# Weights of the second layer split into parts in the first, and attention scores with the other sign

## The chip, the cores and the metric

The kernel runs on one core of one Trainium2 chip. The metric is the device time of one execution in microseconds; before the change it is 2969.87 us, the median of 3 runs (2965.07 to 2971.68).

## The reference, cut to what matters

One inference step of a hybrid decoder: a layer with a Mamba-2 mixer and an MLP, then a shared projection to keys and values, then a layer with attention and an MLP. There are 1104 tokens in one pass: 1024 of a prompt, 64 of samples (8 sequences of 8) and 16 meta tokens; the second layer has 1088, without the meta tokens. All inputs are fp32.

```python
D_MODEL = 1024; D_FF = 4096; WINDOW = 128        # 16 query heads of 64, 4 key/value heads

def sq_relu_mlp(h, norm_w, w_up, w_down):
    return h + jnp.square(jax.nn.relu(rmsnorm(h, norm_w) @ w_up)) @ w_down

def shared_kv(h, kv_norm_w, w_kv):
    return (rmsnorm(h, kv_norm_w) @ w_kv)         # split into keys and values

def queries(h, norm_w, w_q):
    return (rmsnorm(h, norm_w) @ w_q)

def sink_softmax(scores, mask, sinks):            # one learned score per head beside the keys
    s = jnp.where(mask, scores, -jnp.inf)
    return jax.nn.softmax(jnp.concatenate([s, sink], axis=-1), axis=-1)[..., :-1]

# layer 0: h = h + mamba_mixer(h); h = sq_relu_mlp(h, ...)
# layer 1: hp = hp + swa_prompt(q_p, k_p, v_p, ...) @ w_o   (scores = q k * 64 ** -0.5, window of 128)
#          hs = hs + swa_sample(...) @ w_o ; h = sq_relu_mlp(h, ...) ; final rmsnorm
```

## The kernel before

**Products of fp32.** TensorE (PE) multiplies a rounded form of fp32 (fp32r). For full precision each operand is held as two such parts, high and low, and `mm3` (L174) issues three matmuls for each slice of 128: high by high, high by low, low by high (L179, L180, L181). The activations stay in SBUF as parts. The weights come from DRAM as units of 128x1024 numbers (512 KB), and each use of a unit makes its parts anew. `wunit` (L156) does this: a raw tile is loaded by a DMA of the SP queue (L160), GpSimd (POOL) multiplies it with the weights of the norm where the unit has them (L162), ScalarE (ACT) casts it to the high part (L164), and POOL subtracts that from the raw tile, which gives the low part (L165). Raw tiles come from a ring of 2 (L168), part tiles from a ring of 6 (L172), which the whole kernel shares.

**First layer, MLP.** After the mixer and two pairs of columns of the plain kind (`plain_up`, L858), `up` (L972) runs over 14 pairs `f` of column blocks of w_up. Each pair goes through Strassen's scheme, 7 products instead of 8 (`up_pair`, L913): `up_weights` (L894) loads two raw units, forms sums and differences on VectorE (DVE, L900, L906) and splits each of the seven into parts with `wparts` (L887: ACT L890, POOL L891), one slot of the ring of 6 for each. One raw tile in three comes from a slot of its own (`raw2`, L880). Then come one plain `down_block` and `down_blocks` (L1034): four blocks `b` of rows of w_down, each with four column blocks `p` of seven products `i`; between the products `step` loads and splits what the next block needs.

**Second layer, attention.** Keys and values are made from 4 units of w_kv (`keys`, L1186, `values`, L1220), with a raw load, a multiplication, a cast and a subtraction each. `attention` (L1414) then goes over three chunks of tokens, two pairs of heads `pr` and four `r`: `queries` (L1269) multiplies one unit of w_q, so that each of the 8 units is loaded and split three times, once a chunk; `attn_block` (L1313) handles 128 queries of two heads. In it PE makes the scores of each head in `sc`, DVE scales them by `rsq`, adds the mask and takes the maximum with the sink in one instruction (L1328, which writes `es` and, as an accumulator, the maximum into `few`). `soft` (L1295) changes the sign of the maxima (L1300, DVE, 128x2), ACT takes the exponentials with the negative maximum as bias and sums them (L1302), DVE takes the reciprocal (L1303) and multiplies (L1306); PE transposes the result, DVE and ACT copy it out of PSUM (`mb` L1343, `pb` L1345), PE multiplies with the values (`yb`), and ACT and DVE split the result into parts `ah` and `al` (L1356, L1357). `out_unit` (L1478) multiplies the attention output with units of w_o, 8 units three times each; DVE adds the product to the stream (L1490 from PSUM, L1491 from SBUF). At the end come the second layer's first two pairs of w_up, again by `plain_up` with `wunit`, then `up` and `down_blocks` as before.

**What sets the order.** The program is written as loops, and the framework's scheduler orders the instructions of all engines by its own estimate of their times. Each engine then takes its instructions in that order, and so does the SP queue that issues all the DMAs: an instruction that waits for a slot or a result holds all behind it on its engine.

## Time and profile before

| | |
|---|---|
| median of 3 runs | 2969.87 us (2965.07 to 2971.68) |
| profiled execution | 2972.13 us |
| its span, first to last instruction | 2970.4 us |
| mean granted clock of TensorE | 0.982 |
| busy: PE, DVE, ACT, POOL | 2848.8, 1945.4, 1452.5, 1419.9 us |

The stages in the profiled execution, in us from the start of the span: mixer and the first plain columns up to 1107, `up` of the first layer to 1407, its plain `down_block` to 1455 and `down_blocks` to 1722; keys and values 1725 to 1830, attention to 2211, the last output units and the start of the second MLP to 2300, and the rest of that MLP to the end.

The clock given for a stretch is the mean of what PE was granted in it, 1.00 being 2.4 GHz. "Busy" of PE counts overlapping matmuls once. Behind a group of instructions stands the idle time of its engine just before them, with the instruction that ended most of it.

### The profile page before, as it was taken

The numbers are of one execution on the slowest core, as the hardware profiler recorded it, in microseconds if no ns is written. First come the engines' busy times: TensorE is split into PE (matmuls) and PEld (weight loads), VectorE is DVE, ScalarE is ACT, GpSimd is POOL, SyncE is SP. The second block draws the span as 40 slices with busy tenths as digits, with TensorE's granted clock in tenths as the row PEclk, the third lists the DMA queues.
The fourth block names the chain that finished last, engine by engine and source line by source line (L and its number), as shares of the span: only waits on it lengthen the run. The fifth ranks groups of instructions, "written<-read, shape, count | busy, mean of one in ns | idle before, by whom it ended". The sixth has DMA issues, their size and how long they took to land.

```text
span 2970.4 us, 50898 instructions
## 1 busy us (share of the span) xinstructions
PE 2848.8 (96%) x19751; PEld 2733.9 (92%) x19751; DVE 1945.4 (65%) x3150; ACT 1452.5 (49%) x2771; POOL 1419.9 (48%) x1251
## 2 busy tenths in 40 slices
PE   8999999989999989999999999998988999999998
PEld 6999999979999989999999998887878999999998
DVE  6788777775646665453666766776788545366675
ACT  6555555555544554545333336555655444433333
POOL 5566666663223134444355555464543444435562
PEclk9999999999999999999999999998998999999999
DMA  4344444443212224445433312132233344543332
GB/s 134 97 127 125 123 123 124 132 128 117 65 58 88 82 81 158 136 151 181 189 129 129 119 43 65 59 93 89 88 108 103 133 140 145 192 167 127 132 108 75
DMA packets 195609, 346.38 MB, mean 117 GB/s; under 512 B 26712, under 2 KB 128984, under 8 KB 192792
## 3 DMA queue, kind: packets, MB, share of 16 engines
q1 hardware_dynamic: 195368, 343.14, 36.0%
q8 instruction: 155, 2.54, 0.4%
q14 instruction: 86, 0.70, 0.1%
HBM read 252.93 MB, written 91.12 MB: 116 GB/s over the span
## 4 chain that ended last, share of the span: by engine, by line
PE 37%; DVE 12%; DMA 5%; ACT 4%; issue 4%; POOL 3%; DVEq 0%; ACTq 0%; POOLq 0%; SPq 0%
PE g L179 4%; PE g L180 4%; PE g L181 4%; PE mc L179 2%; PE mc L181 2%; PE mc L180 2%; PE ma L179 2%; PE ma L180 2%; PE ma L181 2%; DMA t_e<-rx 2%; POOL w L891 2%; PE md L181 2%; PE md L180 2%; PE md L179 2%; PE mb L180 2%
## 5 line engine op out<-in xcount | busy, mean ns | idle before, releaser
L165 POOL TENSOR_TENSOR w<-raw,w 128x1024 fp32r<-128x1024 f32 x140 | 352.9, 2523 | 437.5 <-ACT w L164 355.3
L179 PE MATMUL g<-S,w 128*128 128x384 f32 (+2 forms) x1584 | 535.3, 338 | 14.1 <-DVE hh L761 4.8
L180 PE MATMUL g<-S,w 128*128 128x384 f32 (+2 forms) x1584 | 534.5, 337 | 0.1
L181 PE MATMUL g<-S,w 128*128 128x384 f32 (+2 forms) x1584 | 531.1, 336 | 2.0 <-POOL w L165 2.0
L891 POOL TENSOR_TENSOR w<-s,w 128x384 fp32r<-128x384 f32 (+1 forms) x240 | 321.7, 1343 | 396.7 <-ACT w L890 394.7
L891 POOL TENSOR_TENSOR w<-raw,w 128x384 fp32r<-128x384 f32 (+1 forms) x180 | 227.6, 1267 | 228.0 <-ACT w L890 205.0
L179 PEld LDWEIGHTS g<-S,w 128*128 128x128 f32 x1584 | 302.1, 191 | 18.9 <-DVE hh L761 5.1
L181 PEld LDWEIGHTS g<-S,w 128*128 128x128 f32 x1584 | 302.2, 191 | 3.5 <-POOL w L165 2.3
L180 PEld LDWEIGHTS g<-S,w 128*128 128x128 f32 x1584 | 302.3, 191 | 1.8 <-issue 0.7
L890 ACT CAST w<-s 128x384 fp32r<-128x384 f32 (+1 forms) x240 | 134.4, 562 | 233.4 <-PE ma L181 82.0
L179 PE MATMUL ma<-S,w 128*128 128x276 f32 (+1 forms) x736 | 214.6, 292 | 9.8 <-DVE us L1091 6.6
L180 PE MATMUL ma<-S,w 128*128 128x276 f32 (+1 forms) x736 | 213.7, 290 | 0.9 <-DVE S L855 0.9
L181 PE MATMUL ma<-S,w 128*128 128x276 f32 (+1 forms) x736 | 213.7, 290 | 0.0
L164 ACT CAST w<-raw 128x1024 fp32r<-128x1024 f32 x140 | 146.4, 1046 | 106.1 <-PE g L180 40.6
L568 DVE SCALAR_TENSOR_TENSOR fm<-xp,cv,fm 128x1024 f32<-128x1024 f32 x96 | 161.1, 1680 | 33.1 <-ACT fm L549 32.5
L761 DVE TENSOR_TENSOR hh<-hh,g 128x384 f32<-128x384 f32 (+2 forms) x264 | 134.4, 531 | 68.6 <-PE g L181 68.1
L890 ACT CAST w<-raw 128x384 fp32r<-128x384 f32 (+1 forms) x180 | 100.3, 561 | 148.7 <-PE mc L181 49.1
L179 PEld LDWEIGHTS ma<-S,w 128*128 128x128 f32 x736 | 139.9, 190 | 11.3 <-issue 5.2
L180 PEld LDWEIGHTS ma<-S,w 128*128 128x128 f32 x736 | 140.0, 190 | 1.1 <-DVE S L855 1.1
L181 PEld LDWEIGHTS ma<-S,w 128*128 128x128 f32 x736 | 139.8, 190 | 0.0
L179 PE MATMUL mc<-S,w 128*128 128x276 f32 (+1 forms) x464 | 134.6, 290 | 2.1 <-DVE hh L1091 1.3
L181 PE MATMUL mc<-S,w 128*128 128x276 f32 (+1 forms) x464 | 134.0, 289 | 0.0
(483 smaller groups left out, 8944.6 us busy)
## 6 DMA issues: line engine op xcount, KB each, us to landing
raw<-in_w_up_dram SPq DMA_DIRECT2D x64, 512.0 KB
raw<-in_w_in_dram SPq DMA_DIRECT2D x48, 512.0 KB
raw<-in_w_downs_dram SPq DMA_DIRECT2D x64, 384.0 KB
ab<-acs_d SPq DMA_DIRECT2D x64, 256.0 KB
S<-t_d SPq DMA_DIRECT2D x18, 828.0 KB
S<-t_e SPq DMA_DIRECT2D x18, 816.0 KB
t_d<-rx SPq DMA_DIRECT2D x12, 1104.0 KB
t_e<-rx SPq DMA_DIRECT2D x12, 1088.0 KB
```

The lines of the kernel that those rows point to most:

```text
L164: nc.scalar.copy(out=wh, in_=raw)
L165: nc.gpsimd.tensor_tensor(out=wl, in0=raw, in1=wh.bitcast(F32), op=ALU.subtract)
L179: mm(out=out, lhsT=wh, rhs=xh, start=(first and k == 0), stop=False)
L180: mm(out=out, lhsT=wh, rhs=xl, start=False, stop=False)
L181: mm(out=out, lhsT=wl, rhs=xh, start=False, stop=(k == n - 1))
L568: nc.vector.scalar_tensor_tensor(out=acc[:, :SEQ], in0=xp[:, k:k + SEQ], scalar=cv[:, j, k:k + 1], in1=acc[:, :SEQ], op0=ALU.mult, op1=ALU ...
L761: nc.vector.tensor_tensor(out=hv, in0=hv, in1=pt[:, :n], op=ALU.add)
L890: nc.scalar.copy(out=t[:, 0], in_=src)
L891: nc.gpsimd.tensor_tensor(out=t[:, 1], in0=src, in1=t[:, 0].bitcast(F32), op=ALU.subtract)
```

## The change

Two things are changed. First, 24 units of the second layer (8 of w_q, 4 of w_kv, the first 4 of w_up, 8 of w_o) are made into parts once, in the first layer's MLP: `split_ahead` calls `wunit` for the next unit of a list, and writes both parts to DRAM. It is called 14 times in `up`, after each pair, and 10 times in `down_blocks`, after the last product of the first three column blocks of a block, as long as the list lasts. In the second layer `wunit` loads both parts into slots of the ring of 6, in two DMAs of 512 KB, and does nothing else; there are 56 such uses. Second, the scores are computed with the other sign: `rsq`, the scale of the sample's scores and the sink are negative, the mask sum takes the minimum, and the exponential has a scale of -1, so that the minimum is already the bias. The instruction of L1300 is gone (68 times).

```diff
-    def wunit(self, view, a, b, pre=None, to=None):
-        nc = self.nc
+    def wunit(self, view, a, b, pre=None, to=None, key=None):
+        nc = self.nc
+        if key in self.split:
+            ws = [self.wtile([P, a, b]) for _ in range(2)]
+            for e, w in enumerate(ws):
+                nc.sync.dma_start(out=w.bitcast(F32), in_=self.split[key][:, e].rearrange("p (a b) -> p a b", b=b))
+            return ws
         raw = self.raw([P, a, b])
...
         return wh, wl
+    def split_ahead(self, n=1):
+        nc = self.nc
+        for key, view, pre in self.ahead[:n]:
+            a = view.shape[1]
+            b = 1024 // a
+            if pre is not None:
+                pre = self.ncol(pre).rearrange("p (k o) -> p k o", o=1).broadcast_to([P, a, b])
+            ws = self.wunit(view, a, b, pre)
+            d = self.dram.tile([P, 2, 1024], F32, name="ws_%s" % "_".join(map(str, key)))
+            for e, w in enumerate(ws):
+                nc.sync.dma_start(out=d[:, e].rearrange("p (a b) -> p a b", b=b), in_=w.bitcast(F32))
+            self.split[key] = d
+        self.ahead = self.ahead[n:]
...
-    def plain_up(self, layer, fp, chs, rd, rs=None, pre=None):
-        nc = self.nc
-        ws = [self.wunit(self.i["w_up"][layer, 2 * fp + e], KT, P, pre) for e in range(2)]
+    def plain_up(self, layer, fp, chs, rd, rs=None):
+        nc = self.nc
+        ws = [self.wunit(self.i["w_up"][layer, 2 * fp + e], KT, P, key=("up", 2 * fp + e) if layer else None)
+              for e in range(2)]
         for c in chs:
...
                 self.up_pair(layer, f, rd, rt)
+                self.split_ahead()
                 if f == 8:
...
                     step(b, p, i)
+                    if i == 6 and p < 3:
+                        self.split_ahead()
...
         nc.sync.dma_start(out=sraw, in_=i["attn_sinks"].broadcast_to([P, 16]))
-        nc.vector.tensor_copy(out=self.sink, in_=sraw.rearrange("p (c h r) -> p c r h", c=2, h=2))
+        nc.vector.tensor_scalar(out=self.sink, in0=sraw.rearrange("p (c h r) -> p c r h", c=2, h=2), scalar1=-1.0,
+                                scalar2=None, op0=ALU.mult)
...
         ks = self.ks[pr] = ap.tile([P, 80], F32, name="ks%d" % pr)
-        wh, wl = self.wunit(i["w_kv"][pr], KT, P, pre=self.kvn)
+        wh, wl = self.wunit(i["w_kv"][pr], KT, P, key=("kv", pr))
         for c, (o, n) in enumerate(CH):
...
         ds = slice(pr * P, pr * P + P)
-        wh, wl = self.wunit(i["w_kv"][2 + pr], KT, P, pre=self.kvn)
+        wh, wl = self.wunit(i["w_kv"][2 + pr], KT, P, key=("kv", 2 + pr))
         for c, (co, n) in enumerate(CH):
...
         o, n = chs[c]
-        wh, wl = self.wunit(i["w_q"][pr, r], KT, P,
-                            pre=self.ncol(1).rearrange("p (k o) -> p k o", o=1).broadcast_to([P, KT, P]))
+        wh, wl = self.wunit(i["w_q"][pr, r], KT, P, key=("q", pr, r))
         qp = at.tile([P, 2, 384], F32R, tag="qp", bufs=2, name="qp")
...
         m, den = sm[:, 0, :], sm[:, 1, :]
-        nc.vector.tensor_scalar(out=m, in0=m, scalar1=-1.0, scalar2=None, op0=ALU.mult)
         for h, e in enumerate(segs):
-            nc.scalar.activation(out=e, in_=e, func=AF.Exp, bias=m[:, h:h + 1], accum_out=den[:, h:h + 1])
+            nc.scalar.activation(out=e, in_=e, func=AF.Exp, scale=-1.0, bias=m[:, h:h + 1],
+                                 accum_out=den[:, h:h + 1])
         nc.vector.reciprocal(out=den, in_=den)
...
                                            scale=self.rsq[:, t:t + 1], scalar=self.sink[:, pr, r, h:h + 1],
-                                           op0=ALU.add, op1=ALU.max, accum_out=sm[:, 0, h:h + 1])
+                                           op0=ALU.add, op1=ALU.min, accum_out=sm[:, 0, h:h + 1])
         self.soft(sm, es[:, :w], [es[:, :w + 1, h] for h in range(2)])
...
             nc.vector.tensor_tensor_reduce(out=es[:, h, :208], in0=sc[:, :208],
-                                           in1=self.mask8[:, 80 * half:80 * half + 208], scale=0.125,
-                                           scalar=self.sink8[:, pr, h:h + 1], op0=ALU.add, op1=ALU.max,
+                                           in1=self.mask8[:, 80 * half:80 * half + 208], scale=-0.125,
+                                           scalar=self.sink8[:, pr, h:h + 1], op0=ALU.add, op1=ALU.min,
                                            accum_out=sm[:, 0, h:h + 1])
...
         nc = self.nc
-        ws = [self.wunit(self.i["w_o"][pr, v], 4, 256) for pr in prs]
+        ws = [self.wunit(self.i["w_o"][pr, v], 4, 256, key=("o", pr, v)) for pr in prs]
         last = prs[-1] == 1
...
         self.gpos = 0
+        i = self.i
+        self.split = {}
+        self.ahead = [(("q", pr, r), i["w_q"][pr, r], 1) for pr in range(2) for r in range(4)]
+        self.ahead += [(("kv", j), i["w_kv"][j], 0) for j in (0, 2, 1, 3)]
+        self.ahead += [(("up", j), i["w_up"][1, j], 3) for j in range(4)]
+        self.ahead += [(("o", pr, v), i["w_o"][pr, v], None) for pr in range(2) for v in range(4)]
         self.dram = self.pool("dram", space=DRAM)
...
                 ps = self.pool("psat", bufs=1, space=PSUM, ctx=c1)
-                self.kvn = self.ncol(0).rearrange("p (k o) -> p k o", o=1).broadcast_to([P, KT, P])
                 self.kk, self.kl, self.ks = {}, {}, {}
...
                 self.more_banks(ce, 5, 0)
-                pre = self.ncol(3).rearrange("p (k o) -> p k o", o=1).broadcast_to([P, KT, P])
-                plain = self.plain_up(1, 0, {c: chs[c] for c in (0, 2, 1)}, rd, stream.rs, pre)
+                plain = self.plain_up(1, 0, {c: chs[c] for c in (0, 2, 1)}, rd, stream.rs)
                 next(plain)
...
                         step(i, k)
-                for _ in self.plain_up(1, 1, {c: chs[c] for c in (0, 2, 1)}, rd, stream.rs, pre):
+                for _ in self.plain_up(1, 1, {c: chs[c] for c in (0, 2, 1)}, rd, stream.rs):
                     pass
```

**POOL in `up`.** POOL's order in the first layer's `up`: before, one pair `f` and the start of the next; `w` is the part tile, `s` a sum, `raw` a loaded unit, and each row is one or more subtractions of `wparts`.

```order
L891 TENSOR_TENSOR w<-raw,w 128x512 x2
L891 TENSOR_TENSOR w<-s,w 128x512
L891 TENSOR_TENSOR w<-raw,w 128x512
L891 TENSOR_TENSOR w<-s,w 128x512 x3
L891 TENSOR_TENSOR w<-raw,w 128x512 x2
```

The same stretch after (L912 is the subtraction of `wparts`, L167 and L170 are the multiplication and the subtraction of `wunit`):

```order
L912 TENSOR_TENSOR w<-raw,w 128x512
L912 TENSOR_TENSOR w<-s,w 128x512 x3
L912 TENSOR_TENSOR w<-raw,w 128x512 x2
L912 TENSOR_TENSOR w<-s,w 128x512
L167 TENSOR_TENSOR raw<-raw,nv 128x1024
L170 TENSOR_TENSOR w<-raw,w 128x1024
L912 TENSOR_TENSOR w<-raw,w 128x512
L912 TENSOR_TENSOR w<-s,w 128x512
L167 TENSOR_TENSOR raw<-raw,nv 128x1024
```

Between the products' parts now stand the 128x1024 multiplication and subtraction of the split ahead, one of each for a pair.

**SP in attention.** The SP queue near the middle of the attention of the first chunk, before (`raw` is the tile that POOL and ACT make parts of; `h_e` is the stream on its way to DRAM):

```order
L160 DMA raw<-in_w_q_dram 128x1024 x5
L160 DMA raw<-in_w_o_dram 128x1024 x2
L160 DMA raw<-in_w_q_dram 128x1024
L1246 DMA out_dram<-vt 128x128
L160 DMA raw<-in_w_o_dram 128x1024
L1244 DMA vm<-vt 16x64 x2
L1248 DMA out_dram<-vt 8x128 x8
L160 DMA raw<-in_w_o_dram 128x1024
L160 DMA raw<-in_w_q_dram 128x1024
L160 DMA raw<-in_w_o_dram 128x1024
L111 DMA h_e<-hs 128x384 x2
L160 DMA raw<-in_w_o_dram 128x1024
```

And after (L162 is the load of a part; `ws_q` and `ws_o` are the units' parts in DRAM):

```order
L162 DMA w<-ws_q_0_12888 128x1024 x2
L162 DMA w<-ws_q_1_13132 128x1024 x2
L162 DMA w<-ws_q_2_13376 128x1024 x2
L162 DMA w<-ws_q_3_13624 128x1024 x2
L162 DMA w<-ws_q_0_11912 128x1024 x2
L162 DMA w<-ws_q_1_12156 128x1024 x2
L162 DMA w<-ws_o_0_16025 128x1024 x2
L1271 DMA out_dram<-vt 128x128
L162 DMA w<-ws_o_0_17113 128x1024 x2
L1269 DMA vm<-vt 16x64 x2
L1273 DMA out_dram<-vt 8x128 x8
L162 DMA w<-ws_q_2_12400 128x1024 x2
L162 DMA w<-ws_o_1_16389 128x1024 x2
```

Each unit is now two loads into `w` tiles, in the place of one into `raw`.

**SP behind `up`.** The SP queue at the end of the first layer's `up`, before (`hh` is the stream, loaded for the plain `down_block`, whose weights are w_down):

```order
L160 DMA raw<-in_w_down_dram 128x1024
L961 DMA t_d_110<-n_14284 128x552
L963 DMA t_d_110<-rx 512x1x552
L965 DMA t_d_110<-n_14377 128x552
L970 DMA t_d_110<-o_14479 128x276
L970 DMA t_d_110<-o_14482 128x276
L160 DMA raw<-in_w_down_dram 128x1024
L956 DMA r_d_105<-rx 128x2208
L160 DMA raw<-in_w_down_dram 128x1024
L990 DMA hh<-h_d 128x1104 x8
L1015 DMA raw<-in_w_downs_dram 128x768
L160 DMA raw<-in_w_down_dram 128x1024
```

And after (`ws_up` is a unit of w_up whose parts are written):

```order
L184 DMA ws_up_14837<-w 128x1024 x2
L165 DMA raw<-in_w_up_dram 128x1024
L977 DMA r_d_105<-rx 128x2208
L165 DMA raw<-in_w_down_dram 128x1024
L184 DMA ws_up_15072<-w 128x1024 x2
L1012 DMA hh<-h_d 128x1104 x8
L165 DMA raw<-in_w_down_dram 128x1024 x2
L1037 DMA raw<-in_w_downs_dram 128x768
L1076 DMA S<-t_d_107 128x1656 x5
L1037 DMA raw<-in_w_downs_dram 128x768
L977 DMA r_d_106<-rx 128x2208
L165 DMA raw<-in_w_down_dram 128x1024
```

The loads of w_down that stood ahead of the eight loads of `hh` now stand behind them, but for the first.

## Rows read from the trace of the kernel before

**Rows 1.** The page's first part: busy us, share of the span, instructions, by engine

```profile
PE 2848.8 (96%) x19751; PEld 2733.9 (92%) x19751; DVE 1945.4 (65%) x3150; ACT 1452.5 (49%) x2771; POOL 1419.9 (48%) x1251
```

**Rows 2.** Five stretches: us, busy PE, PEld, DVE, ACT, POOL, clock, DMA share, GB/s

```profile
1107.00:1407.00 300.00, 298.31 (x2338) 297.64 (x2338) 145.89 (x187) 145.79 (x240) 130.70 (x96) 1.00 0.44 153
1455.00:1722.00 267.00, 254.49 (x1955) 253.31 (x1954) 172.91 (x191) 91.72 (x138) 146.27 (x115) 0.98 0.35 121
1725.00:1830.00 105.00, 100.68 (x608) 98.40 (x608) 69.51 (x106) 53.63 (x92) 62.27 (x57) 1.00 0.20 59
1830.00:2211.00 381.00, 354.40 (x2478) 313.91 (x2479) 286.38 (x740) 227.82 (x605) 191.11 (x158) 0.96 0.25 77
2211.00:2300.00 89.00, 75.50 (x414) 73.02 (x411) 78.64 (x96) 41.66 (x62) 27.49 (x13) 0.87 0.39 132
```

**Rows 3.** Groups by line, 1725 to 2300: busy us, mean ns, idle before

```profile
L165 POOL TENSOR_TENSOR w<-raw,w 128x1024 fp32r<-128x1024 f32 x59 | 145.9, 2476 | 87.5 <-ACT w L164 68.1 <-DVE mb L1343 8.1 <-DVE few L1328 2.8
...
L162 POOL TENSOR_TENSOR raw<-raw,nv 128x1024 f32<-128x1024 f32 x32 | 64.4, 2013 | 62.2 <-DMA raw<-in_w_q_dram 32.4 <-DMA raw<-in_w_up_dram 14.1 <-DMA raw<-in_w_kv_dram 11.4
L164 ACT CAST w<-raw 128x1024 fp32r<-128x1024 f32 x58 | 60.6, 1045 | 44.2 <-PE g L180 20.4 <-POOL raw L162 17.6 <-PE mc L181 3.5
...
L1306 DVE TENSOR_TENSOR es<-es,few 128x544 f32<-128x544 f32 x56 | 49.4, 882 | 0.8
...
L1300 DVE TENSOR_SCALAR few<-few 128x2 f32<-128x2 f32 x68 | 37.8, 556 | 0.8
...
L1491 DVE TENSOR_TENSOR hs<-hs,S 128x384 f32<-128x384 f32 x16 | 16.8, 1052 | 0.2
```

**Rows 4.** Waits, 1725 to 2300, PE then ACT: us in total, times, longest

```profile
PE g L179 <- DVE X L1490: 7.7, 2, 4.7
PE yb L1348 <- DVE mb L1343: 4.1, 5, 1.4
PE yb L1335 <- DVE es L1306: 3.8, 2, 3.5
...
PE yb L1335 <- ACT es L1302: 1.8, 1, 1.8
...
ACT es L1302 <- DVE few L1300: 42.0, 27, 3.3
```

**Rows 5.** Four lines of DVE in attention: ns min/median/max, first and last start

```profile
L1300 DVE TENSOR_SCALAR few<-few x67: 145/169/2364, 1832.7 to 2204.2; 128x2 f32<-128x2 f32 x67
...
L1303 DVE RECIPROCAL few<-few x67: 150/166/169, 1835.4 to 2206.5; 128x2 f32<-128x2 f32 x67
...
L1306 DVE TENSOR_TENSOR es<-es,few x68: 453/724/2920, 1828.7 to 2206.7; 128x544 f32<-128x544 f32 x56, 128x288 f32<-128x288 f32 x8, 128x416 f32<-128x416 f32 x4
...
L1490 DVE TENSOR_TENSOR hs<-g,S x24: 476/545/558, 1956.2 to 2188.1; 128x384 f32<-128x384 f32 x16, 128x320 f32<-128x320 f32 x8
```

**Rows 6.** Timeline, 2012.8 to 2017.2, DVE and POOL: start, us, instruction, idle before

```profile
2012.89 1.92 POOL L162 TENSOR_TENSOR raw<-raw,nv 128x1024 f32<-128x1024 f32 x1 [1.32 <-DMA raw<-in_w_q_dram]
...
2013.35 1.49 DVE L1300 TENSOR_SCALAR few<-few 128x2 f32<-128x2 f32 x1
...
2016.18 1.92 POOL L162 TENSOR_TENSOR raw<-raw,nv 128x1024 f32<-128x1024 f32 x1 [1.37 <-DMA raw<-in_w_q_dram]
...
2017.04 1.50 DVE L1306 TENSOR_TENSOR es<-es,few 128x416 f32<-128x416 f32 x1
```

**Rows 7.** Timeline of the SP queue, same place: start, us, transfers

```profile
2009.23 2.69 SPq L160 DMA_DIRECT2D raw<-in_w_q_dram  x2
```

**Rows 8.** Timeline in `up`, 1260.3 to 1263, ACT and POOL

```profile
1260.73 0.62 ACT L890 CAST w<-s 128x512 fp32r<-128x512 f32 x1 [0.95 <-PE ma L181]
...
1261.43 1.55 POOL L891 TENSOR_TENSOR w<-s,w 128x512 fp32r<-128x512 f32 x1 [1.75 <-ACT w L890]
```

**Rows 9.** Timeline of the SP queue at the end of `up`

```profile
1397.85 0.33 SPq L160 DMA_DIRECT2D raw<-in_w_down_dram  x1
1398.27 5.79 SPq L990 DMA_DIRECT2D hh<-h_d  x8
```

More of the change, by code (lines that the diff above doesn't have):

```diff
@@ L1265, in query_norms @@
             nc.tensor.transpose(pt[:, t:t + 1], xs.rs[c][0:1, o:o + P], self.ident[0:1, 0:1])
-        nc.vector.tensor_scalar(out=self.rsq, in0=pt[:, 0:8], scalar1=0.125, scalar2=None, op0=ALU.mult)
+        nc.vector.tensor_scalar(out=self.rsq, in0=pt[:, 0:8], scalar1=-0.125, scalar2=None, op0=ALU.mult)
         nc.vector.tensor_copy(out=self.rss, in_=xs.rs[2][:, 256:320])
```

## The prediction, made before the changed kernel ran

> **What bounds the kernel now.** I read the busy shares first [rows 1]: TensorE (PE) is busy 2848.8 of 2970.4 us, so only about 120 us of PE idle time, and the time in which PE runs at half its clock, can be taken away. Next the stages [rows 2]. In the first layer's `up` (1107 to 1407 us) PE is busy 298.31 of 300 us at a granted clock of 1.00: nothing is to be had there, and whatever is added can only cost. In `down_blocks` of the first layer (1455 to 1722) it is 254.49 of 267 at 0.98. The holes are in the second layer: keys and values 100.68 of 105, attention 354.40 of 381 at 0.96, the last output units with the start of the MLP 75.50 of 89 at 0.87. A mean granted clock of 0.96 between the levels of 1.2 and 2.4 GHz means that some matmuls ran at the lower one; I price it as (1 − clock) × stretch. What is lost is then, in attention, 381 − 354.40 = 26.6 us idle and 0.04 × 381 = 15.2 us of clock, 41.8 together; in the stretch behind it 13.5 + 0.13 × 89 = 25.1; in keys and values 4.3. **About 71 us is the most that these stages can give back.**
>
> Then why PE waits there. The groups of 1725 to 2300 us [rows 3] show GpSimd (POOL) making the weight parts: 59 subtractions of 2476 ns (145.9 us) and 32 multiplications of 2013 ns (64.4 us), with casts on ScalarE (ACT) between. PE hardly waits for those parts. It waits for the softmax chain of VectorE (DVE) and ACT [rows 4], 4.1 us for `mb`, 3.8 and 1.8 for `es`, and for the adds that empty the output units, 7.7 us in two waits for L1490's `X`. ACT itself waits 42.0 us, 27 times, for the change of sign at L1300, an operation on 128x2 numbers.
>
> That operation tells the story [rows 5]: 145 ns at best, 169 at the median, 2364 at worst; 37.8 us in 68 calls [rows 3]. The reciprocal at L1303, of the same size, never takes more than 169 ns. The timeline shows what holds it [rows 6]: L1300 begins at 2013.35 and lasts 1.49 us, to 2014.84; POOL's multiplication runs 2012.89 + 1.92 = 2014.81. L1306 begins at 2017.04 and lasts until 2018.54, and POOL's next one ends at 2018.10. L1306 has a mean of 882 ns and a median of 724; L1491 has 1052 where L1490, of the same size but with one operand in PSUM, has 545 at the median and 558 at most. **DVE is stretched by POOL.** In attention, L1300 gives up 37.8 us at once, L1306 about 56 × (882 − 724) = 9 and L1491 about 16 × (1052 − 545) = 8: some 55 of DVE's 286.38 us.
>
> **The change, part by part.** *Scores negated.* Sixty-eight DVE instructions go, and with them one step in each block's chain between the minimum and ACT's exponential. ACT's scale and the minimum in place of the maximum cost nothing that I can see: the same instructions on the same elements; the trace of before shows neither form, and other reductions and scales there suggest zero.
>
> *Parts loaded in the second layer.* 56 unit uses (24 q, 4 kv, 24 o, 4 up) lose a raw load of 512 KB, a cast of 1045 ns on ACT, a subtraction of 2476 ns and, for 32 of them, a multiplication of 2013 ns on POOL: 56 × 2.48 + 32 × 2.01 = 203 us of POOL's 281 in the three stages of the second layer in rows 2. They gain a second DMA of 512 KB. DMA stands at 0.25 of its engines' time in attention and would go to 0.4 or so. In order: the SP queue now holds 2 loads per unit, and each waits for a slot of the ring of six `w` tiles, thus 3 units; before, two raw tiles stood ahead of that ring. A raw load issued at 2009.23 let POOL begin at 2012.89 [rows 6, 7], 3.66 us. A pair takes between 3.7 (both at once) and 7.3 us (one behind the other) plus 0.7 for two issues; I take 5, since DMA is mostly free. A unit has 24 matmuls, by the mean of the keys and values 24 × 100.68 / 608 = 4.0 us, so two units ahead last 8 us, and attention blocks often lie between. So I cost them at 0; if pairs cost 7.3 and other transfers stand ahead, two units no longer cover them (a rival, below).
>
> What comes back? The waits on the softmax chain shrink by L1300 (0.56 us a block, up to 2.4) and by the stretch of L1306; with gaps of 2 us and more go the half-clock spells behind them. DVE falls from 75% to about 60% of attention, no longer near PE's own pace where a step has no output unit. I take two thirds of 41.8, **28 us**. The bounds: only the waits named, 4.1 + 3.8 + 1.8, with the same share of the clock's 15.2, about 15, or all 41.8. In the last stretch the long waits are for norm and output blocks on DVE (L1490, 7.7 us), whose chain stays in place and only loses its stretch: 40% of 25.1, **10 us**, bounds 3 and 25. Keys and values: **1 us** of 4.3.
>
> *The splits in the first layer.* 14 units in `up`, one per pair `f`, 10 in `down_blocks`. Each adds a raw load, a cast of 1.05 us on ACT, 2.48 us of POOL (4.49 with the norm weights, 16 units) and two writes of 512 KB. In `up` POOL goes from 130.7 to about 131 + 14 × 4.5 = 194 of 300 us and DMA from 153 GB/s to 153 + 14 × 1.57 MB / 300 us = 226. What counts is lead. The slot that PE leaves when the product ends at about 1260.6 is cast at 1260.73 and subtracted until 1261.43 + 1.55 = 1262.98 [rows 8]; a product lasts 298.31 / 2338 × 24 = 3.06 us, and five products stand between, so PE comes to it at 1275.9: lead 12.9 us. A split takes two of the six slots until its writes have landed, leaving three products, 9.2 us, less the 2.4 of preparation: 6.8. If the split's own 4.5 us of POOL and 1.05 of ACT stand just ahead, 1.3. Still positive, so **0 in `up`** when all goes as ordered. The third raw tile is the weak point: one pair in three has its first raw behind the previous pair's last sum, which may take 2 to 3 us off the lead; five pairs at up to 1.5 us is my bound, 8. Between `up` and `down_block`, the raw loads of w_down, which stood at 1397.85 ahead of the eight loads of `hh` [rows 9], now stand behind them. Those eight took 5.79 us to issue, to 1404.1; `up` ends near 1407, and a load issued then takes 3.7 us and waits behind what the eight move: 0 to 4 us. In `down_blocks` the lead is five products of 18 × 254.49 / 1955 = 2.3 us less some 2 of preparation; a split's POOL work of 2.5 to 4.5 us stands ahead of the next products, and its raw load waits for the split before: 0 to 2 us each for ten. Together 0 to 32; I take **6**, near the lower end because each lead stays positive by rows 8.
>
> **Sum.** −28 − 10 − 1 + 6 = −33. The profiled execution took 2972.1 us (span 2970.4), 2.3 above the median of the runs shown (2969.9), so 2972.1 − 33 − 2.3 = **2937 us** as a median.
>
> **Rivals.** *(a) Slower: the leads in the first layer break.* For: three products of lead, raw rotation and an SP queue in which the writes wait for POOL in front of the next raw loads. Against: 6.8 us of lead worked out above, and POOL busy for only two thirds. The point is a delay of more than 7 us for a pair. Then each pair waits about 2.5 us and PE loses some 1.7 us of clock behind it: 14 × 4.2 = 59, and ten splits of 2 us are 20; against −39 this gives +40, 3010 us. Half as many waits give 2970 to 2975.
>
> *(b) Same: the loads become the wait.* If pairs take 7.3 us and wait in the queue behind others, 28 of 56 unit uses at 1.2 us lose 34 us, and the time is near 2969. Against: 8 us of PE work ahead of each, and more where blocks lie between.
>
> *(c) Small gain: PE, DVE and ACT go on in turn.* Only the lower bounds come back, 15 us in attention and 3 behind it, less 6 and the offset: 2958. For: ACT is busy 228 of 381 us, and much of the chain (exp, transposes, copies) is untouched.
>
> *(d) Larger gain.* Nearly all 71 us return and the first layer costs nothing: 2900. For: half-clock spells follow the gaps, so both go together.
>
> *(e) The stretch only moves.* In rows 6, DVE is held as long as the POOL instruction lasts; in `up` 63 us of new POOL work meet DVE's `s` sums and differences. If each new microsecond stretched DVE as in attention (55 of 191 us, 0.29), `up` would have 18 us more DVE work and `down_blocks` 8. DVE is busy 146 of 300 us in `up`, so most of this hides; with half on PE's path, the time would be 2937 + 13 = 2950. The Trainium skill (SBUF — State Buffer, section "SBUF: two separate sides") says that DVE and GpSimd contend for an exclusive lock on a shared port pair, that the one that starts first keeps it for its whole instruction, and that an operation with two SBUF inputs is held too; by that rule the contention goes wherever POOL's work goes, which speaks against the change. The trace agrees as to L1300 and L1306 and as to L1490, which is not held.
>
> **Chances.** Forecast (2915 to 2947) 0.52; (e) 0.08; (c) 0.10; (d) 0.12; (b) 0.07; (a) 0.11. Faster by over 0.2% (about what a measurement can tell here, 6 us): 0.52 + 0.08 + 0.10 + 0.12 = 0.82; within it 0.07; slower 0.11. The range reaches 2902 to 2966: it leaves out half of (d), some of (b) and most of (a).
>
> **What would show it.** Right: L1300 gone; L1306's mean near 724 and L1491's near 550; DVE in attention near 230 of its stretch; PEclk above 0.98 there; POOL nearly idle; `up` still 298 of 300 us. Wrong: PE waits for `w` from DMA in attention (b); waits of PE for L891 or L890 in 1107 to 1722, or a clock under 1.00 there (a); DVE far lower but PE still waiting for `mb` and `es` (c); the `s` sums at L900 longer than now (e).

## The result and the profile after

The changed kernel takes 2944.51 us (median of 4 runs, 2940.96 to 2946.87), the kernel before 2969.64 on the same chip (4 runs). The ratio is 0.9916, with a 95% interval of 0.9899 to 0.9934: **25 us faster**, where 33 were forecast. The profiled execution has a span of 2942.1 us, 28.3 below the 2970.4 of before.

The net hides two larger numbers. The table gives the length of each stage in the two traces, in us: `up` and `down_blocks` from their first to their last matmul, attention from its first to its last product of scores, and the other stages what lies between.

| stage | before | after | difference | forecast |
|---|---|---|---|---|
| first layer, start to `up` | 1105.2 | 1105.7 | +0.5 | 0 |
| `up`, first layer | 301.9 | 326.3 | **+24.4** | 0 (bound 8) |
| plain `down_block` | 48.5 | 48.4 | −0.1 | 0 to 4 |
| `down_blocks`, first layer | 274.7 | 279.9 | +5.2 | 0 to 20 |
| keys and values | 94.3 | 89.2 | −5.1 | −1 |
| attention | 378.1 | 336.7 | **−41.4** | −28 |
| last output units, start of the MLP | 82.1 | 74.2 | −7.9 | −10, with the next row |
| `up`, second layer | 305.9 | 301.1 | −4.8 | |
| the rest | 379.7 | 380.4 | +0.7 | 0 |

The second layer gave back 59 us where 39 were forecast, and the first layer cost 30 where 6 were. First the stretches of after, the view of [rows 2] (length, then busy us of PE, PEld, DVE, ACT and POOL, granted clock, DMA share, GB/s): `up`, `down_blocks`, keys and values, attention, and what lies behind it.

```profile
1105.50:1432.00 326.50, 309.06 (x2354) 306.15 (x2353) 186.70 (x188) 156.81 (x254) 196.18 (x123) 0.98 0.59 205
1480.00:1760.00 280.00, 266.25 (x2017) 264.57 (x2016) 183.02 (x195) 102.02 (x150) 181.78 (x130) 0.96 0.49 174
1760.00:1849.00 89.00, 88.43 (x533) 87.81 (x532) 47.76 (x94) 43.31 (x76) 24.30 (x39) 1.00 0.30 94
1849.00:2186.00 337.00, 333.17 (x2462) 303.15 (x2461) 224.33 (x668) 190.58 (x558) 39.25 (x92) 1.00 0.49 159
2186.00:2260.00 74.00, 68.64 (x412) 66.43 (x413) 58.95 (x101) 33.10 (x57) 5.90 (x1) 0.98 0.45 157
```

In attention PE is now busy 333.17 of 337 us at a clock of 1.00; before it was 354.40 of 381 at 0.96. POOL fell from 191 us to 39, DVE from 286 to 224. In `up`, where PE was busy 298.31 of 300 us at 1.00, it now lacks 17 us and has a clock of 0.98; POOL went from 131 to 196 us as forecast, but DVE went from 148 to 187 over the whole of `up`, although the change adds no DVE instruction there.

The lines of [rows 5] in attention after (ns min/median/max): L1331 is the multiplication that was L1306, L1516 the add that was L1491, L1515 that of L1490. L1491 before stands behind them, with its spread.

```profile
L1331 DVE TENSOR_TENSOR es<-es,few x66: 449/722/1145, 1853.8 to 2184.3; 128x544 f32<-128x544 f32 x54, 128x288 f32<-128x288 f32 x8, 128x416 f32<-128x416 f32 x4
...
L1516 DVE TENSOR_TENSOR hs<-hs,S x24: 472/556/918, 1971.5 to 2174.7; 128x384 f32<-128x384 f32 x16, 128x320 f32<-128x320 f32 x8
L1515 DVE TENSOR_TENSOR hs<-g,S x24: 485/554/559, 1970.9 to 2173.8; 128x384 f32<-128x384 f32 x16, 128x320 f32<-128x320 f32 x8
```

```profile
L1491 DVE TENSOR_TENSOR hs<-hs,S x24: 491/834/2800, 1956.8 to 2188.7; 128x384 f32<-128x384 f32 x16, 128x320 f32<-128x320 f32 x8
```

The maximum of the multiplication fell from 2920 ns to 1145, and the add over SBUF now has the median of the add over PSUM (834 ns before). With 39 us of POOL left, DVE is hardly held any more. In `up` PE's waits for `mc` are new (us in total, times, longest; before, 0.4 us in one), and ACT waits longer for the landing of `rx`. First PE, then ACT, and behind them ACT's wait for the landing before:

```profile
PE mc L199 <- DVE rx L941: 16.6, 11, 2.8
PE ma L199 <- ACT n L957: 0.8, 1, 0.8
...
ACT n L957 <- DMA t_d<-n: 48.9, 11, 6.4
ACT rx L974 <- DVE rx L941: 33.5, 17, 4.0
ACT rx L959 <- DMA t_d<-rx: 31.1, 12, 3.8
```

```profile
ACT rx L938 <- DMA t_d<-rx: 17.5, 12, 2.6
```

PE does not wait for a part of a weight. It waits for DVE to add a product into `rx` and so to free the PSUM bank `mc`. One such wait, in the timeline after (start, us, instruction, idle before and its releaser):

```profile
1205.41 1.53 POOL L912 TENSOR_TENSOR w<-s,w 128x512 fp32r<-128x512 f32 x1 [0.21 <-ACT w L911]
...
1205.82 1.71 DVE L979 TENSOR_TENSOR rx<-rx 128x552 f32<-128x552 f32 x1
...
1207.56 0.52 SPq L984 DMA_DIRECT2D t_d<-rx  x1
...
1215.40 0.62 ACT L959 COPY rx<-md 128x552 f32<-128x552 f32 x1 [3.68 <-DMA t_d<-rx]
...
1216.05 0.73 DVE L941 TENSOR_TENSOR rx<-mc,rx 128x552 f32<-128x552 f32 x1 [3.75 <-ACT rx L959]
...
1216.84 0.40 PE L199 MATMUL mc<-S,w 128*128 128x276 f32 x1 [1.60 <-DVE rx L941]
```

`rx` holds the results of a pair and has one buffer. DVE's difference of the pair before starts while POOL's subtraction runs (to 1206.94) and takes 1.71 us, which is its mean after (1706 ns, 1141 before); SP issues the write of `rx` when it ends; the buffer is free when that has landed, 7.8 us after its issue; only then may ACT copy the next result into it, DVE add to it, and PE write `mc` again. The same chain before:

```profile
1199.50 0.73 DVE L958 TENSOR_TENSOR rx<-rx 128x552 f32<-128x552 f32 x1
...
1200.26 0.53 SPq L963 DMA_DIRECT2D t_d<-rx  x1
...
1205.91 0.62 ACT L938 COPY rx<-md 128x552 f32<-128x552 f32 x1 [2.56 <-DMA t_d<-rx]
```

There the difference takes 0.73 us, and ACT copies 5.7 us after the issue of the write. So the hold of the difference is the smaller part of what this chain grew by: over the 12 pairs it is 0.57 us longer on average, and the time from the issue of the write to ACT's copy 2.2 us longer at the median (4.8 before, 6.9 after). In the case shown SP issued two raw loads from 1203.97 to 1205.55, just ahead of the write; before, the last one was issued at 1195.50. Whether these loads make the write later was not tried.

### The profile page after: what moved, and what is told of

Same layout as the page of the kernel before. It is cut to its first block, busy times and chain, and to the rows that moved or that the text cites. A ratio compares the mean times of both kernels' runs of the same rounds, so it can differ in the third digit from the quotient of the medians.

```text
span 2942.1 us, 51007 instructions
## 1 busy us (share of the span) xinstructions
PE 2836.2 (96%) x19751; PEld 2729.6 (93%) x19751; DVE 1900.4 (65%) x3082; ACT 1430.5 (49%) x2739; POOL 1318.3 (45%) x1203
## 2 busy tenths in 40 slices
DMA packets 214043, 413.51 MB, mean 141 GB/s; under 512 B 28761, under 2 KB 131033, under 8 KB 211225
## 4 chain that ended last, share of the span: by engine, by line
PE 43%; DMA 6%; DVE 6%; issue 5%; ACT 3%; POOL 2%; SPq 0%; POOLq 0%; DVEq 0%; ACTq 0%
PE g L199 5%; PE g L200 5%; PE g L201 5%; PE mc L199 2%; PE mc L201 2%; PE ma L199 2%; PE mc L200 2%; PE ma L201 2%; PE ma L200 2%; PE mb L199 2%; PE mb L200 2%; PE mb L201 2%; PE md L201 2%; PE md L200 2%; POOL w L912 2%
## 5 line engine op out<-in xcount | busy, mean ns | idle before, releaser
L912 POOL TENSOR_TENSOR w<-s,w 128x384 fp32r<-128x384 f32 (+1 forms) x240 | 325.5, 1362 | 325.5 <-ACT w L911 317.6
L170 POOL TENSOR_TENSOR w<-raw,w 128x1024 fp32r<-128x1024 f32 x108 | 274.2, 2541 | 423.8 <-ACT w L169 344.6
L912 POOL TENSOR_TENSOR w<-raw,w 128x384 fp32r<-128x384 f32 (+1 forms) x180 | 232.7, 1300 | 195.5 <-ACT w L911 178.7
L169 ACT CAST w<-raw 128x1024 fp32r<-128x1024 f32 x108 | 113.1, 1048 | 107.4 <-DMA raw<-in_w_o_dram 18.5
L199 PE MATMUL mc<-S,w 128*128 128x276 f32 (+1 forms) x464 | 138.3, 298 | 17.9 <-DVE rx L941 16.6
L201 PE MATMUL mc<-S,w 128*128 128x276 f32 (+1 forms) x464 | 136.6, 294 | 0.0
```

The costliest lines, as they stand in the source:

```text
L169: nc.scalar.copy(out=wh, in_=raw)
L170: nc.gpsimd.tensor_tensor(out=wl, in0=raw, in1=wh.bitcast(F32), op=ALU.subtract)
L199: mm(out=out, lhsT=wh, rhs=xh, start=(first and k == 0), stop=False)
L201: mm(out=out, lhsT=wl, rhs=xh, start=False, stop=(k == n - 1))
L912: nc.gpsimd.tensor_tensor(out=t[:, 1], in0=src, in1=t[:, 0].bitcast(F32), op=ALU.subtract)
```

## The experiments

**Each half alone.** The kernel before with the negative scores and nothing else:

```diff
-        nc.vector.tensor_scalar(out=m, in0=m, scalar1=-1.0, scalar2=None, op0=ALU.mult)
-            nc.scalar.activation(out=e, in_=e, func=AF.Exp, bias=m[:, h:h + 1], accum_out=den[:, h:h + 1])
+            nc.scalar.activation(out=e, in_=e, func=AF.Exp, scale=-1.0, bias=m[:, h:h + 1],
+                                 accum_out=den[:, h:h + 1])
...
```

> The scores negated alone, on the kernel before: L1300 is gone, every unit is still split at each use. If the gain of the second layer comes from POOL no longer holding DVE, the next DVE instruction with two SBUF inputs is held in L1300's place: the mean of the multiplication after the reciprocal stays near 880 ns or grows, and the time falls by 0 to 12 us (2958 to 2970). If it comes from the step taken out of the softmax chain (ACT's 42 us of waiting for L1300), most of the second layer's 59 us comes back here: 2925 to 2945. The first layer stays as before (its `up` 302 us from first to last matmul).

Measured: 2942.46 us against 2963.23, ratio 0.9927 (0.9909 to 0.9944). **This half alone gains nearly what the whole change gains.** Attention takes 349.4 us instead of 378.1. The time is that of the second expectation, though only half of the second layer's 59 us come back; what the first said of the instructions is right, and its time is wrong. Attention of this kernel, first the stretch, then groups by line (busy us, mean ns | idle before), then two waits of ACT:

```profile
1827.00:2176.00 349.00, 338.55 (x2459) 304.68 (x2457) 263.61 (x670) 230.34 (x606) 194.34 (x158) 1.00 0.28 87
```

```profile
L1307 DVE TENSOR_TENSOR es<-es,few 128x544 f32<-128x544 f32 x55 | 51.9, 943 | 1.2
L1492 DVE TENSOR_TENSOR hs<-hs,S 128x384 f32<-128x384 f32 x16 | 19.6, 1223 | 0.3
```

```profile
ACT es L1302 <- DVE few L1329: 26.3, 30, 3.3
ACT S L1493 <- DVE hs L1492: 21.4, 12, 3.9
```

POOL is as busy as before (194 us), and the hold did move on in part: the multiplication went from 882 to 943 ns, the add from 1052 to 1223. These are 3 us each, against the 37.6 of L1300 that are gone; DVE's sum fell from 285 to 264 us. Of the 37.6, 11.8 are what the instruction takes without POOL's splits (the next run), so some 26 us were hold; all other DVE instructions together take 12 us more than before. Nearly half of the hold moved to them, and the rest found no instruction to hold. With what is left PE loses less: the gaps of 2 us and more are gone, and the granted clock is 1.00 instead of 0.96. That an instruction on the way to ACT's exponential costs more than one behind it would explain this; no run separates it from the hold that is gone.

The other half, with L1300 kept:

```diff
+        nc.vector.tensor_scalar(out=m, in0=m, scalar1=-1.0, scalar2=None, op0=ALU.mult)
-            nc.scalar.activation(out=e, in_=e, func=AF.Exp, scale=-1.0, bias=m[:, h:h + 1],
-                                 accum_out=den[:, h:h + 1])
+            nc.scalar.activation(out=e, in_=e, func=AF.Exp, bias=m[:, h:h + 1], accum_out=den[:, h:h + 1])
...
```

> The parts made ahead and loaded, with the old sign: L1300 stays, 68 times. If POOL's hold is the cause, L1300 takes about 170 ns each without POOL's work (12 us for all instead of 37.8) and the second layer keeps 50 or more of its 59 us; the time is 2944 to 2955. If the step in the chain is the cause, the second layer gives back less than 25 us, and with the 30 us lost in the first layer the time is 2975 or more.

Measured: 2949.12 against 2963.23, ratio 0.9949 (0.9934 to 0.9964). Attention takes 336.5 us, as with both halves (336.7). The line of the sign (busy us, mean ns):

```profile
L1324 DVE TENSOR_SCALAR few<-few 128x2 f32<-128x2 f32 x67 | 11.8, 176 | 0.9
```

176 ns where it had 556 [rows 3]: with little of POOL beside it, this instruction costs 12 us of DVE, and attention is no longer for it. So in attention the two halves are two ways to much the same gain, 28.7 and 41.6 alone and 41.4 together, since PE's own 333 us of work end it. The loads take the casts off ACT too (its 227.82 us [rows 2] became 190.58 with the change); what that is worth beside the hold, no run separates. The parts alone pay 30 us or more in the first layer for it (`up` 324.4, `down_blocks` 284.5).

**Another place for the splits.** All 24 in the mixer's output product:

```diff
                     gx.append(list(self.gate_group(g + 1, xs))[-1])
-                    self.down(self.i["w_out"][g], 2, gx[g], hts, CH)
+                    self.split_ahead(2)
+                    self.down(self.i["w_out"][g], 2, gx[g], hts, CH, step=lambda u: self.split_ahead())
...
                 self.up_pair(layer, f, rd, rt)
-                self.split_ahead()
...
-                    if i == 6 and p < 3:
-                        self.split_ahead()
```

> All 24 splits moved ahead of the MLP, into the loop over six groups of the mixer's output product (two after each gate group, one after each of its two weight units), with the rest of the change as it is. If the first layer's 30 us are a matter of where the splits stand (a stage with POOL, DVE and DMA less loaded), `up` is back at 302 us and `down_blocks` at 275, the mixer's output takes 0 to 10 us more, and the time is 2912 to 2925, below both kernels. If the splits cost the same wherever they are made (about 1.2 us each), the time stays at 2940 to 2948.

Measured: 2950.51 against 2963.23, ratio 0.9952 (0.9934 to 0.9969). `up` is back at 304.0 and `down_blocks` at 272.2, but `up` begins at 1140.3 instead of 1105.2: the splits cost 35 us there, 1.5 each. The first expectation was wrong, and the second, 1.2 us each, was too low: a POOL that is busy a third of a stage was no free place. From 600 us to the start of `up`, before and in this kernel:

```profile
600.00:1105.00 505.00, 480.99 (x2845) 467.93 (x2844) 308.55 (x534) 263.33 (x413) 165.95 (x98) 0.98 0.28 87
```

```profile
600.00:1140.00 540.00, 495.06 (x2844) 478.14 (x2843) 330.08 (x534) 287.17 (x437) 255.62 (x138) 0.96 0.46 152
```

DVE has the same 534 instructions and 21.5 us more, PE the same work, 21 us more idle time and a clock of 0.96.

**Which part of a split costs.** In `up`, two kernels that leave one part out, each executed once. Without POOL:

```diff
-            ws = self.wunit(view, a, b, pre)
+            raw = self.raw([P, a, b])
+            nc.sync.dma_start(out=raw, in_=view)
+            ws = [self.wtile([P, a, b]) for _ in range(2)]
+            for w in ws:
+                nc.scalar.copy(out=w, in_=raw)
```

> The change with POOL left out of the splits: the raw load, two casts on ACT and both writes stay, the multiplication by the norm weights and the subtraction are left out, so that the parts are not those of the weights. Three causes for the 24.4 us that `up` got longer. Held DVE (the added POOL work stretches the sums and differences whose results PE waits for): `up` is back at 302 to 308 us. DMA (the writes and raw loads delay the landing of the pair's results): `up` stays at 318 to 328. Slots (the ring of w): unchanged too, 320 or more.

Measured: `up` takes 308.4 us, `down_blocks` 273.4, and the one time is 2922.16. **Without POOL's part of the splits 17.9 of the 24.4 us are gone.** Groups of DVE by line in `up` (busy us, mean ns), the sums of the weights (L921 after, L925 here; before they had 835 and 760 ns) and the differences of the results (1141 before), in the changed kernel and in this one:

```profile
L921 DVE TENSOR_TENSOR s<-raw 128x512 f32<-128x512 f32 x26 | 30.7, 1208 | 17.0 <-DMA raw<-in_w_up_dram 17.0
L921 DVE TENSOR_TENSOR s<-raw,s 128x512 f32<-128x512 f32 x14 | 21.7, 1549 | 15.2 <-POOL w L912 14.6
L979 DVE TENSOR_TENSOR rx<-rx 128x552 f32<-128x552 f32 x12 | 20.5, 1706 | 0.4
```

```profile
L925 DVE TENSOR_TENSOR s<-raw 128x512 f32<-128x512 f32 x26 | 17.2, 690 | 25.6 <-DMA raw<-in_w_up_dram 25.6
L925 DVE TENSOR_TENSOR s<-raw,s 128x512 f32<-128x512 f32 x14 | 14.0, 998 | 8.0 <-POOL w L916 7.0
L983 DVE TENSOR_TENSOR rx<-rx 128x552 f32<-128x552 f32 x12 | 16.6, 1380 | 0.3
```

Without the writes, with POOL's work as in the change:

```diff
-            d = self.dram.tile([P, 2, 1024], F32, name="ws_%s" % "_".join(map(str, key)))
-            for e, w in enumerate(ws):
-                nc.sync.dma_start(out=d[:, e].rearrange("p (a b) -> p a b", b=b), in_=w.bitcast(F32))
-            self.split[key] = d
+            if not self.split:
+                self.d = self.dram.tile([P, 2, 1024], F32, name="ws")
+                for e, w in enumerate(ws):
+                    nc.sync.dma_start(out=self.d[:, e].rearrange("p (a b) -> p a b", b=b), in_=w.bitcast(F32))
+            self.split[key] = self.d
```

> The change with the writes left out for 23 of the 24 units: all the splits are made as in the change, only the first unit's parts are written, and the second layer loads these for every unit, so that its products are those of other weights. If POOL's hold on DVE makes `up` longer, `up` stays at 318 to 326 us (302 before, 326.3 with the change); if the writes' traffic does, it falls to 302 to 310. Attention stays at 336 to 338 us.

Measured: `up` takes 320.7 us, `down_blocks` 281.7, one time of 2940.19. Without the writes 5.6 us of `up` are gone, without POOL's work 17.9; together 23.5 of 24.4, by one trace each. Neither run tells of the slots of the ring alone, since a slot is held for less time in both; in the changed kernel ACT waits 13.2 us in `up` for writes to free a slot, and PE never waits for a part. In the kernel without the writes the difference into `rx` is as short as before the change (1135 ns), the sums are as long as with it (1275 and 1639 ns), and ACT copies into `rx` 7.1 us after the issue of its write at the median: that `up` is longer does not hang on the hold of the difference.

The same work on DVE instead of POOL:

```diff
-            ws = self.wunit(view, a, b, pre)
+            ws = self.wunit(view, a, b, pre, eng=nc.vector)
...
-        nc.gpsimd.tensor_tensor(out=wl, in0=raw, in1=wh.bitcast(F32), op=ALU.subtract)
+        (eng or nc.gpsimd).tensor_tensor(out=wl, in0=raw, in1=wh.bitcast(F32), op=ALU.subtract)
```

> The change with the multiplication and the subtraction of the 24 splits on DVE instead of POOL. DVE gets some 24 x 1.3 + 16 x 1.3 = 50 us of work more in the first layer, of which it is busy for half; POOL gets none. If the mutual hold of POOL and DVE is the cause of the first layer's 30 us, `up` takes 306 to 314 us, `down_blocks` 274 to 278, and the time is 2922 to 2932 on a kernel before of 2965. If it is any added work on the sums' path, `up` stays above 320 and the time at 2938 or more.

Measured: 2928.97 against 2966.55, ratio 0.9874 (0.9859 to 0.9889), **below both kernels**. `down_blocks` takes 272.7 us, no more than before. `up` takes 317.1, 3 us above what was expected, with as much DVE time as in the changed kernel (190 us busy) and shorter waits:

```profile
1105.00:1422.00 317.00, 304.10 (x2352) 300.11 (x2351) 189.95 (x216) 157.41 (x255) 137.20 (x97) 1.00 0.60 210
```

```profile
PE ma L199 <- ACT n L957: 7.7, 8, 2.0
PE mc L199 <- DVE rx L941: 5.2, 10, 0.7
```

The waits are at most 2.0 us and the clock stays at 1.00. So a split costs time in `up` on DVE too, but 9.2 us less for all 14 than on POOL, with as much DVE time: the sum of DVE's time alone does not set the length of `up`.

**No splits in the first layer at all.** The parts of the 16 units that are used three times (w_q, w_o) are made at their first use, as before, and written then; the other uses load them:

```diff
+        if key in self.pre and key[0] in "qo":
+            d = self.split[key] = self.dram.tile([P, 2, 1024], F32, name="ws_%s" % "_".join(map(str, key)))
+            for e, w in enumerate((wh, wl)):
+                nc.sync.dma_start(out=d[:, e].rearrange("p (a b) -> p a b", b=b), in_=w.bitcast(F32))
         return wh, wl
...
                 self.up_pair(layer, f, rd, rt)
-                self.split_ahead()
```

> Nothing is split in the first layer: the units of w_q and w_o are made into parts at their first use in the second layer, as in the kernel before, and written to DRAM there; the other two chunks load the parts. Units of w_kv and w_up, used once, are split at their use. Scores negative. The first layer is back at 302 + 48.5 + 274.5 us. If POOL's work in attention is what matters, a third of it is left: attention 340 to 352 us (378 before, 349 with the negative scores alone, 337 with the change), and the time is 2925 to 2938 on a kernel before of 2965; below both kernels. If 349 us is where any POOL work leaves it, the time is that of the negative scores alone, 0.993 of before.

Measured: 2926.91 against 2966.55, ratio 0.9866 (0.9849 to 0.9883). The first layer is back (301.9, 48.5, 273.4); attention takes 342.1, keys and values 94.4, the stretch behind attention 78.6. Attention of this kernel:

```profile
1828.00:2170.00 342.00, 336.42 (x2466) 303.51 (x2466) 236.73 (x671) 201.81 (x572) 86.65 (x112) 1.00 0.52 175
```

With 87 us of POOL in place of 191 attention is 5.4 us longer than the changed kernel's, and the 30 us of the first layer are saved.

Last, this kernel with the 8 units that are used once split ahead on DVE in `down_blocks`, as in the two edits above.

> As the kernel that makes the parts of w_q and w_o at their first use, and the 8 units that are used once (w_kv and the first four of w_up) split ahead in the first layer's `down_blocks`, with the multiplication and the subtraction on DVE. If what a split costs in the first layer is DVE time in `up` alone, `down_blocks` stays at 272 to 275 us (272.7 with ten such splits on DVE there), keys and values fall from 94.4 to about 89 and the last stretch from 78.6 to 75; the time is 8 us below that kernel's, ratio to before about 0.984. If any split in the first layer costs about 1 us, nothing is left of it: 0.9866 again.

Measured: 2924.12 against 2968.73, ratio 0.9849 (0.9833 to 0.9866): the fastest kernel of this study, but its interval overlaps that of the kernel before it (0.9849 to 0.9883). Keys and values fell to 89.5 and the stretch behind attention to 75.6, as expected; `down_blocks` rose from 273.4 to 279.3, which was not. The second expectation is nearer: 8 splits cost 6 us and gave 8. In the kernel with all splits on DVE ten of them stood at the same places for 272.7; what differs is that here the first eight are multiplied with norm weights, while eight of those ten were w_o, without. That this is the cause was not tried.

## Why the prediction was right or wrong

**The range and the direction held; two terms were wrong, with opposite signs.**

*Attention, −28 forecast, −41.4 measured.* The mechanism was right: DVE held by POOL [rows 6], with L1300 as its main victim, and stretches at half the clock behind the gaps. The step that was mis-sized is the share that comes back, "two thirds of 41.8". All of it came back: PE is busy 333.17 of 337 us at 1.00. The upper bound was the better guess: either half alone removes most of what PE lost. That the halves overlap, the prediction did not see: it gave the sign's removal no price of its own, and by itself it is worth 0.9927.

*Behind attention, −10 forecast, −7.9 and −4.8 measured,* and *keys and values, −1 forecast, −5.1 measured:* the 4.3 us that PE lacked there are gone.

*The first layer, +6 forecast, +29.6 measured.* This is the step that failed: "still positive, so 0 in `up`". The leads of the weight parts were worked out from [rows 8], and they did stay positive: PE waits for parts in `up` not once. But the lead of the weights was taken for the only thing at stake. The results go through DVE, a write and a single buffer, and the slack of that chain was not looked at. Rival (e) named the main mechanism, DVE held in the first layer by the moved work; it was given 18 us of DVE time in `up` and 0.08 of chance. DVE's time grew from 147.89 us to 186.70, by 39, twice the price. `up` before, as a whole:

```profile
1105.00:1407.00 302.00, 300.31 (x2354) 299.64 (x2353) 147.89 (x188) 147.79 (x243) 131.47 (x97) 1.00 0.44 152
```

Of the 24.4 us, 17.9 go with POOL's work and 5.6 with the writes, which no rival had at a price. That they reach PE through the buffer of `rx` is read from the trace; how much of that is held DVE and how much the later landing stays open. In `down_blocks` the loss is mostly clock: PE idles 13.8 us, 12.5 before [rows 2], at a granted clock of 0.96 instead of 0.98. The rule of the Trainium skill that was cited there (SBUF — State Buffer, "SBUF: two separate sides", an exclusive lock for the whole instruction) agrees with these runs: the hold goes where POOL's work goes, and leaves when it leaves (L1300 176 ns without POOL's splits, 562 with them).

*Rival (a)* came in as to its place, with waits of up to 2.8 us and four stretches at half the clock in `up`, but not by its mechanism (weights or raw tiles late). *Rival (b)* was wrong but for one place: in the second layer PE waits once for a loaded part, 4.6 us for one of w_o behind attention. *Rival (c)* is wrong, and *(d)* is near what the second layer did, where keys and values, attention and the stretch behind it gave back 54 of the 71 us.

*The net* was near by luck: the two errors, −20 and +24, cancel. Of the signs named ahead, those of the gain showed (L1300 gone, means near 724 and 550, DVE near 230, clock above 0.98, POOL nearly idle) but for one, `up` still at 298 of 300 us; and of the signs of trouble a clock below 1.00 in `up`, longer `s` sums, and one wait of PE for a part, 1.9 us in `down_blocks`.

## What to carry to other kernels

When work is moved to a stage whose main engine is full, the wait to look for is not only that of the moved work's own product. Take every engine that the work touches or holds, and follow what else that engine hands on in that stage, to the last buffer. Work that held another engine was paid for on both, and a low busy share of the engine that does it was no sign of free room here (a third, and 35 us for 24 splits). And of a change with two halves run each alone: here the deletion of one instruction of 128x2 numbers gave 0.9927 of the time, 24 splits with 67 MB of traffic 0.9949, and both 0.9916: the two do not add.

## What the runs showed of the hardware

- An instruction on 128x2 numbers from SBUF to SBUF took up to 2364 ns beside POOL, while a reciprocal of the same size, also from SBUF to SBUF, never took more than 169 [rows 5]. Both have one input; why the one is held and the other is not, no run here shows.
- A split of a unit of 128x1024 cost between 0.5 us (10 in `down_blocks` after) and 1.7 us (14 in `up` after) of the whole kernel, and 1.5 in the mixer's output, all of it in stages where POOL was busy at most 65% of the time. With its POOL work on DVE it cost between nothing (10 in `down_blocks`) and 1.1 us (14 in `up`).
- ACT copied into the buffer of `rx` 4.8 us after the issue of its write (1.1 MB) before, 6.9 after, and 7.1 in the kernel that leaves out the writes of the parts, each the median of 12 pairs.
- The change moves 413.51 MB instead of 346.38, and of the 56 loads of 1 MB in the second layer only one made PE wait, with DMA at half of its engines' time there.
